# A gather of 1 MB taken apart: U rows first, V rows later and only where the GELU is not zero

## The chip, the cores and the metric

The kernel runs on one core of one Trainium2 chip. The metric is the device time of one execution in microseconds (us). A core has five engines that run on their own and wait for each other by semaphores: TensorE (PE in the profile; PEld is its weight load), VectorE (DVE), ScalarE (ACT), GpSimd (POOL) and SyncE (SP). Sixteen DMA engines move data between HBM and SBUF. SP issues the plain loads here, POOL the indirect ones (gathers).

## The reference, cut to what matters

Four layers work on 256 tokens of width 1024. Each layer is a token mixer (HGRN2, FoX, Mamba-2 SSD, HGRN2) followed by an expert network (PEER). Per token the expert network picks 16 of 16,384 experts for each of 8 heads; an expert has one row of `u_tab` and one of `v_tab`, 1024 floats each:

```python
top_s, pos = lax.top_k(cand_s, PEER_TOPK)
idx = jnp.take_along_axis(cand_i, pos, axis=-1)
gates = jax.nn.softmax(top_s, axis=-1)
u = jnp.take(u_tab, idx, axis=0)
v = jnp.take(v_tab, idx, axis=0)
act = jax.nn.gelu(jnp.einsum('md,mhkd->mhk', xb, u), approximate=False) * gates
return jnp.einsum('mhk,mhkd->md', act, v)
```

So an expert contributes `GELU(x · u) · gate · v`. Where the GELU is zero, the row of V adds nothing. All is float32. The input of the expert network is a normalised vector times a weight near 7.294.

## The kernel before, in words

The 256 tokens are two tiles of 128; four layers by two tiles make eight stages `s` (0 to 7). A stage has 8 heads with 8 pairs of experts each (`NQ`), so 64 iterations; 512 in all (`i` in the main loop at line 1724). One iteration serves one pair of experts of one head for all 128 tokens of the tile: 256 rows. They come by two gathers, `g` = 0 and 1; each brings 128 rows, one to a partition: 64 tokens by 2 experts, `g` being the half of the tokens. The two tables lie side by side in HBM (`uv`): one row is 8 KB, the 1024 floats of U and then those of V. So a gather is 128 rows of 8 KB, 1 MB.

What an iteration does, in program order:

- `fetches(i)` (line 1560): POOL issues gathers until 7 of them are ahead (7 buffers of 1 MB, `NGB`). A gather waits until its buffer is free, which is when the matmuls of the iteration that used it are over.
- `dot(i, 0)`, `dot(i, 1)` (line 1570): DVE multiplies the U half by the tokens (`XR`) and sums each row: one scalar per partition, in tile `dots`.
- `spread(i)` (line 1596): ACT takes the GELU of the two columns, scales the two diagonals `dg` (the gates on a 128 by 64 pattern `m64`) by it, and PE adds the diagonal times the V half into the sum of this stage, a pair of PSUM banks (`acc`): four matmuls, for two halves of the columns and two `g`.
- `others()` and `products_()`: side work for the next tile, of `side(s)`, in small steps: the mixer, the norms, the query projections of stage `s + 1`. `products_` puts PE work in, `others` its evacuation one iteration later. All of it has to be over at iteration 62 of the stage.
- `route_steps`: DVE's top-16 searches that give the indices (`ix`) and gates (`gs`) of heads to come.

Each engine runs its own queue in program order. Nothing is sorted by a scheduler. Three pools of PSUM exist: `ps` (4 banks), `pj` (2 banks, projections of the side work) and `acc` (2 banks, the sum of the stage). The first steps of a stage's side work read the sum of the stage before from `acc`.

Semaphores of gathers go round: the program gives the gathers eight semaphores by turn, so that a gather also waits for the gather eight before it to have landed.

In the last stage more buffers exist (`END`, line 1544): the mixer's room is free then, and up to 19 gathers are ahead.

Of the kernel before, what the change touches and what calls it, by code (L numbers as in the profile page):

```python
# [10 lines left out]
F32 = mybir.dt.float32  # L11
# [17 lines left out]
NGB = 7  # L29
NRAW = 2  # L30
# [17 lines left out]
SPAN = 56  # L48
MOST = ((3.6, 2), (3.5, 2), (3.5, 2), (3.5, 2), (99, 0), (99, 0), (2.8, 2), (3.5, 2))
# [125 lines left out]
def trunk(ctx: ExitStack, tc: tile.TileContext, d: dict, out: bass.AP):  # L175
# [6 lines left out]
    pjp = ctx.enter_context(tc.tile_pool(name="pj", bufs=2, space=SB))  # L182
    accp = ctx.enter_context(tc.tile_pool(name="acc", bufs=2, space=SB))
# [60 lines left out]
    pe = [0.0]  # L244

# [175 lines left out]
    def project(nm, ub, names):  # L421

        for key in names:
            b = pjp.tile([P, 512], F32, name="pj")
# [6 lines left out]
    def out_project(nm, yT, acc):  # L431

        n = len(yT)
        for g in range(n // 4):
            for e in range(2):
                if g == 0:
                    acc.append(pjp.tile([P, 512], F32, name="pj"))
# [761 lines left out]
    def queries(s):  # L1199
# [32 lines left out]
        def alone():  # L1232

            b = pjp.tile([P, 512], F32, name="pj")
# [32 lines left out]
    def pair(s, g, tokens, QT):  # L1267

        l = s // 2
        b = pjp.tile([P, 512], F32, name="pj")  # L1270
# [29 lines left out]
    def late_queries(p, l):  # L1300
# [19 lines left out]
        for i, g in enumerate(gs):  # L1320
# [3 lines left out]
            def start(g=g, made=made):  # L1324
                made["all"] = pair(2 * l, g, tokens, QT)
# [12 lines left out]
    def tail_queries(s, QT):  # L1338

        ready_ = None  # L1340
        for g in (2, 3):
            steps, evac, score = pair(s, g, xT, QT)
# [13 lines left out]
    def beside(norm, work):  # L1356

        for _ in work:
            next(norm, None)
            yield  # L1360
            if deferred:
                flush()
            next(norm, None)
            yield
# [27 lines left out]

    def route(s, hh):
# [15 lines left out]
        igv = ig.rearrange("p c (q j) -> p c q j", j=2)  # L1409
        places = [(slice(j * 64, j * 64 + 64), g, slice(g * 64, g * 64 + 64), j) for g in range(2) for j in range(2)]  # L1410
# [28 lines left out]
        if (s, hh) == (0, 0):  # L1439
# [13 lines left out]
            for o, g, i, j in places:  # L1453
                vec.tensor_copy(ix[o, g, 0:4], igv[i, 0, 0:4, j])
            got[s, hh] = ix, gs, 4
            yield
            for dv, di, src in sides:
# [15 lines left out]
            for o, g, i, j in places:  # L1473
                vec.tensor_copy(ix[o, g, 4:8], igv[i, 0, 4:8, j])
# [4 lines left out]
        else:  # L1479
# [11 lines left out]
            for o, g, i, j in places:  # L1491
                vec.tensor_copy(gs[o, g], igv[i, :, :, j])
            vec.tensor_copy(ix, gs[:, :, 0])
# [46 lines left out]
    accs = {}  # L1540
    sent = [0]
# [4 lines left out]
    def buffer(n):  # L1546

        return GB[n % NGB] if n < LAST else END[(n - LAST) % len(END)]

    def fetch(n):  # L1550
        (s, hh, q), g = pairs[n // 2], n % 2
# [225 lines left out]
```

## Time and profile before

| what | value |
|---|---|
| time, median of 3 runs | 3115.72 us (3115.51 to 3116.24) |
| the profiled execution | 3115.31 us, its span 3113.5 us |
| granted TensorE clock, mean | 0.906 |
| busy share of the span: PE, PEld, DVE, ACT, POOL | 79%, 37%, 68%, 46%, 39% |
| moved by DMA | 1269.42 MB, 408 GB/s on the mean |
| of it by gathers | 1073.81 MB |

The profile is of one execution. Its parts give the busy time of each engine, the span in 40 slices, the DMA queues, the chain of work that ended last, the costliest groups of instructions, and the DMA issues. Other views cut the span into windows, list waits (who waited, for whom, total, number of times, longest), or list instructions in order of time. Queue q0 holds POOL's gathers, q1 SP's loads. A packet of 4 bytes at the end of each DMA on each of the 16 engines signals completion.

### The profile page before, as it was taken

Reading aid. Unit: us, or ns where it says so; the run is one execution under the profiler, and the core shown is the slowest. Engines: PE = TensorE matmul, PEld = TensorE weight load, DVE = VectorE, ACT = ScalarE, POOL = GpSimd, SP = SyncE. Lnnn points to the kernel's source line nnn. Section 1 sums busy time; section 2 is a strip of 40 time slices with the busy share of each in tenths; the row PEclk is TensorE's granted clock in tenths of the full one; section 3 lists DMA queues with packets and bytes.
Section 4 is the critical chain, followed back from the end, with each engine's and each line's share of the span. In section 5 each row is a group of like instructions: output and inputs, shape, how many; then the busy total and the mean of one; then the engine's idle time right before and its main releaser. Section 6 shows DMA issues by size and latency. Waiting matters only on the chain.

```text
span 3113.5 us, 32398 instructions
## 1 busy us (share of the span) xinstructions
PE 2475.0 (79%) x9490; PEld 1153.5 (37%) x9490; DVE 2109.1 (68%) x5580; ACT 1427.1 (46%) x3915; POOL 1200.0 (39%) x1032
## 2 busy tenths in 40 slices
PE   9889768877689777988778998688777898876555
PEld 4434324333235434444233543243323353342222
DVE  1676666667766858678676777577657667776764
ACT  2354334454344634587334674355433544343332
POOL 0243344334443344333343333334334343445443
PEclk9999989988799988999889999899989999888888
DMA  7799999999999999999999999999999999999998
GB/s 310 286 421 403 421 415 404 421 421 419 416 417 418 416 419 408 419 421 412 420 402 421 394 421 421 401 415 421 421 416 411 402 420 421 414 418 416 421 421 345
DMA packets 175710, 1269.42 MB, mean 408 GB/s; under 512 B 19504, under 2 KB 20144, under 8 KB 21296
## 3 DMA queue, kind: packets, MB, share of 16 engines
q0 software_dynamic: 147456, 1073.81, 83.8%
q1 hardware_dynamic: 28080, 193.55, 15.0%
q8 instruction: 78, 1.28, 0.2%
q14 instruction: 96, 0.79, 0.1%
HBM read 1266.23 MB, written 1.05 MB: 407 GB/s over the span
## 4 chain that ended last, share of the span: by engine, by line
DMA 45%; PE 27%; DVE 10%; issue 9%; ACT 5%; POOL 3%; POOLq 0%; DVEq 0%; ACTq 0%
DMA arena<-in_uv,ix 45%; PE acc L1613 12%; PE pj L248 10%; DVE arena L213 8%; PE ps L248 3%; POOL arena L1552 3%; ACT L226 2%; ACT dg L226 2%; ACT arena L226 1%; PE ps L252 1%; ACT dots L226 1%; DVE si L213 0%; DVE cs L213 0%; DMA raw<-in_ssm 0%; DVE sv L213 0%
## 5 line engine op out<-in xcount | busy, mean ns | idle before, releaser
L1552 POOL DMA_INDIRECT arena<-in_uv,ix x1024 | 1196.0, 1168 | 1883.6 <-PE acc L1613 1297.2
L213 DVE SCALAR_TENSOR_TENSOR arena<-arena 128x1024 f32<-128x1024 f32 (+3 forms) x1282 | 1318.4, 1046 | 750.5 <-DMA arena<-in_uv,ix 698.7
L1613 PE MATMUL acc<-arena,dg 128*64 128x512 f32 x4096 | 1266.9, 708 | 611.6 <-ACT dg L226 610.5
L1613 PEld LDWEIGHTS acc<-arena,dg 128*64 128x64 f32 x4096 | 449.7, 152 | 1245.4 <-ACT dg L226 929.9
L226 ACT ACTIVATE dots<-dots 128x2 f32<-128x2 f32 x512 | 103.3, 202 | 1462.8 <-DVE arena L213 1462.3
L248 PE MATMUL pj<-arena 128*128 128x128 f32 (+1 forms) x1752 | 510.1, 440 | 2.0 <-DVE arena L213 1.2
L226 ACT ACT_TABLE_LOAD x339 | 434.9, 1283 | 6.9 <-DVE arena L213 0.8
L248 PE MATMUL pj<-raw,arena 128*128 128x512 f32 x808 | 387.0, 615 | 11.0 <-DMA raw<-in_ssm 8.3
L248 PEld LDWEIGHTS pj<-arena 128*128 128x128 f32 x1752 | 259.4, 193 | 258.8 <-issue 237.9
L226 ACT ACTIVATE dg<-dg,dots 128x64 f32<-128x64 f32 x1024 | 300.4, 340 | 16.7
L226 ACT ACTIVATE dg<-m,gs 128x64 f32<-128x64 f32 x1024 | 292.5, 333 | 0.0
L248 PEld LDWEIGHTS pj<-raw,arena 128*128 128x128 f32 x808 | 145.6, 193 | 248.7 <-issue 222.1
L248 PE MATMUL ps<-arena 128*128 128x128 f32 (+6 forms) x1120 | 149.7, 287 | 1.2 <-ACT arena L1242 1.2
L248 PEld LDWEIGHTS ps<-arena 128*128 128x128 f32 (+3 forms) x1120 | 117.9, 171 | 77.6 <-issue 46.5
L213 DVE MAX8 sv<-arena 128x8 f32<-128x128 f32 x256 | 62.5, 290 | 38.7 <-ACT arena L1228 22.0
L213 DVE DVE_READ_ACCUMULATOR arena<-arena 128x1 f32 x1024 | 84.5, 83 | 0.0
L252 PEld LDWEIGHTS ps<-fst,arena 128*128 128x128 f32 x504 | 60.6, 147 | 62.3 <-issue 35.8
L252 PE MATMUL ps<-fst,arena 128*128 128x128 f32 x504 | 80.0, 288 | 1.3 <-DVE arena L213 1.3
L226 ACT ACTIVATE arena<-arena 128x128 f32<-128x128 f32 (+2 forms) x133 | 67.0, 546 | 18.0 <-DVE arena L213 15.6
L213 DVE FIND_INDEX8 si<-sv,arena 128x8 uint32<-128x128 f32 x256 | 69.8, 285 | 0.0
L248 PEld LDWEIGHTS ps<-fst,arena 128*64 128x64 f32 (+2 forms) x704 | 56.4, 154 | 15.1 <-issue 8.2
L248 PE MATMUL ps<-cst,arena 128*128 128x128 f32 (+2 forms) x256 | 61.7, 358 | 0.0
(119 smaller groups left out, 1291.6 us busy)
## 6 DMA issues: line engine op xcount, KB each, us to landing
raw<-in_ssm SPq DMA_DIRECT2D x48, 1024.0 KB, 9.3
raw<-in_hg SPq DMA_DIRECT2D x35, 1024.0 KB, 9.5
arena<-in_wq SPq DMA_DIRECT2D x28, 1024.0 KB, 9.5
arena<-in_hg SPq DMA_DIRECT2D x27, 1024.0 KB, 15.9
arena<-in_uv,ix POOLq DMA_INDIRECT x1024, 12.0
raw<-in_fox SPq DMA_DIRECT2D x14, 1024.0 KB, 9.8
arena<-in_fox SPq DMA_DIRECT2D x9, 1024.0 KB, 13.7
raw<-in_wq SPq DMA_DIRECT2D x8, 1024.0 KB, 10.4
```

Source lines behind the costliest of these rows:

```text
L213: return getattr(nc.vector, name)(o, *a, **k)
L226: nc.scalar.activation(o, i, f, **k)
L248: nc.tensor.matmul(o, w, m, start=start, stop=stop)
L252: nc.tensor.transpose(o, i, ident)
L1552: nc.gpsimd.indirect_dma_start(buffer(n), None, d["uv"], bass.IndirectOffsetOnAxis(ap=got[s, hh][0][:, g, q:q + 1], axis=0))
L1613: nc.tensor.matmul(accs[s][e][g * 64:g * 64 + 64], dg[:, g], v, start=False, stop=hh == 7 and q == NQ - 1)
```

## The change

The first gather of an iteration stays as it is. The second (`g` = 1) is taken apart for all but the last four iterations (`apart(i)`, 508 of 512): `fetch(i, 1)` brings U rows alone, 128 rows of 4 KB, from the same table seen as rows of half the length (`halved`). V follows in a third gather, `rest_of(i)`. Its index comes from `ask(i)`: two DVE instructions that read the GELU of column 1 and, where it is exactly zero, add a number (`FAR`) beyond the bound of the table; the gather is given that bound and leaves such rows out. What was in the buffer stays there, and is multiplied by zero. `rest_of(i)` is issued one iteration later, and its rows are added in `spread(i + 3)` (`LAG`), ahead of that iteration's own first rows.

The 14 half buffers are divided anew: four of 8 KB a partition for first gathers, three halves for U and three for V. At the end, the four whole second gathers go to the mixer's room, and `END` is gone. Since the index of a U row is twice that of a whole row, `route` doubles those of `g` = 1.

ACT makes the diagonal of the second half later (`diagonal`), from the product of GELU and gate.

Since a stage's last V rows are added three iterations into the next stage, its sum is needed longer. So the pairs of banks `acc` and `pj` swap roles from stage to stage, and the side work that reads the sum waits until iteration 2 of a stage (`LAG - 1`). Work that needs no sum (the last query projections, `tail_queries`) comes ahead of it in the stages where it exists, and in a few iterations at the start of a stage two steps are taken instead of one (`TWICE`).

```diff
+NW = 4
+NH = 3
+LAG = 3
+FAR = 1 << 18
+TWICE = ((3, 4, 5), (1, 2, 3, 4, 5))
...
+    def pj():
+        return (accp, pjp)[(now[0] // 64 + 1) % 2].tile([P, 512], F32, name="pj")
...
+    def apart(i):
+
+        return i < 64 * STAGES - 4
...
-    LAST = 2 * NQ * 8 * (STAGES - 1) + 2 * 16
-    END = [GB[(LAST + k) % NGB] for k in range(NGB)] + [mix[:, o:o + 2 * D] for o in range(3 * D, MIX - 2 * D + 1, 2 * D)]
...
+    halved = d["uv"].rearrange("e (h d) -> (e h) d", h=2)
+    HALF = [at_["gb"][:, (2 * NW + i) * D:(2 * NW + i + 1) * D] for i in range(2 * NH)]
+    def buffer(i, g):
+
+        if not g:
+            return GB[i % NW]
+        if apart(i):
+            return HALF[i % NH]
+        return mix[:, (3 + 2 * (i % 4)) * D:(5 + 2 * (i % 4)) * D]
...
+    def ask(i):
+
+        s, hh, q = pairs[i]
+        a, w = acts[i], asks.setdefault(i, wk2.tile([P, 1], I32, name="ask", bufs=3))
+        vec.tensor_scalar(a[:, 5:6], a[:, 3:4], 0.0, float(FAR), op0=OP.is_equal, op1=OP.mult)
+        stt(w, a[:, 5:6], 1.0, got[s, hh][1][:, 1, 0, q:q + 1], op0=OP.add, op1=OP.add)
+
+    def rest_of(i):
+
+        nc.gpsimd.indirect_dma_start(HALF[NH + i % NH], None, halved, bass.IndirectOffsetOnAxis(ap=asks.pop(i), axis=0),
+                                     bounds_check=2 * DEPTH * P * P - 1, oob_is_err=False)
...
+        while sent[0] < len(jobs_):
+            i, g = jobs_[sent[0]]
+            if pairs[i][2] >= known(i) or i >= n + (NH if g else NW):
+                break
+            if n - 1 in asks and not g:
+                rest_of(n - 1)
+            fetch(i, g)
+            sent[0] += 1
...
+        act(a[:, 2:4], a[:, 0:2], AF.Gelu)
...
+        if i >= LAG and apart(i - LAG):
+            add_rows(i - LAG, 1)
+        for g in range(1 + two):
+            add_rows(i, g)
...
+        while s and now[0] < 64 * s + LAG - 1:
+            yield "wait"
...
-            new, end = i % 64 == 0 and s > 0, i % 64 == 63 and s + 1 < STAGES
+            new, end = i % 64 in TWICE[s % 2] and s > 0, i % 64 == 63 and s + 1 < STAGES
...
             others()
+            if apart(i):
+                ask(i)
```

Three places show how instructions move. The first is POOL's queue in the middle of the program (`arena<-in_uv` is a gather into a buffer; DMASW is a semaphore of an earlier gather; DVE and PE are waits for those engines). Before, two gathers of 128 by 2048 floats an iteration:

```order
L1552 DMA arena<-in_uv,ix 128x2048 [waits DMASW1_49,DVE_49,PE_49]
L1552 DMA arena<-in_uv,ix 128x2048 [waits DMASW2_49,DVE_49,PE_49]
L1552 DMA arena<-in_uv,ix 128x2048 [waits DMASW3_49,DVE_49,PE_49]
L1552 DMA arena<-in_uv,ix 128x2048 [waits DMASW4_49,DVE_49,PE_49]
L1552 DMA arena<-in_uv,ix 128x2048 [waits DMASW5_49,DVE_49,PE_49]
```

With the change, three an iteration: U of iteration n + 2, V of n - 1 (index `ask`), and the whole rows of n + 3:

```order
L1571 DMA arena<-in_uv,ix 128x1024 [waits DMASW7_49,DVE_49]
L1583 DMA arena<-in_uv,ask 128x1024 [waits DMASW0_49,DVE_49,PE_49]
L1571 DMA arena<-in_uv,ix 128x2048 [waits DMASW1_49,PE_49]
L1571 DMA arena<-in_uv,ix 128x1024 [waits DMASW2_49,DVE_49]
L1583 DMA arena<-in_uv,ask 128x1024 [waits DMASW3_49,DVE_49,PE_49]
L1571 DMA arena<-in_uv,ix 128x2048 [waits DMASW4_49,PE_49]
```

The gather of U needs no wait for PE any more, since its buffer is free after the dot product; the gather of V waits for DVE's `ask`, and the whole rows of n + 3 stand behind it. There are 1,024 gathers before, and 1,532 now.

The second place is DVE's queue in one iteration with routing work. Before (the two 128x1024 instructions are the dot products):

```order
L213 TENSOR_TENSOR cs<-cs,sf 128x512 [waits DVE_49]
L213 SCALAR_TENSOR_TENSOR arena,dots<-arena 128x1024 [waits DMASW4_49]
L213 SCALAR_TENSOR_TENSOR arena,dots<-arena 128x1024 [waits DMASW5_49]
L213 TENSOR_TENSOR st<-st 128x1 [waits Activation_49]
L213 TENSOR_REDUCE af<-cs 128x32 [waits DVE_49]
```

With the change, in an iteration with the same routing work:

```order
L218 TENSOR_TENSOR cs<-cs,sf 128x512 [waits DVE_49]
L218 SCALAR_TENSOR_TENSOR arena,dots<-arena 128x1024 [waits DMASW3_49]
L218 SCALAR_TENSOR_TENSOR arena,dots<-arena 128x1024 [waits DMASW4_49]
L218 TENSOR_TENSOR arena<-pj,arena 128x512 [waits PE_49] x2
L218 TENSOR_SCALAR dots<-dots 128x1 [waits Activation_49]
L218 SCALAR_TENSOR_TENSOR ask<-dots,gs 128x1 [waits DMASW5_49,DVE_49]
L218 TENSOR_REDUCE af<-cs 128x32
```

The two new instructions of `ask` stand behind the side work's evacuation (here two additions that wait for PE) and ahead of the routing; they wait for ACT.

The third place is PE's queue. Before, two iterations with side work between them:

```order
L1613 MATMUL acc<-arena,dg 64x512 [waits DMASW0_49,Activation_49]
L1613 MATMUL acc<-arena,dg 64x512 [waits DMASW1_49,Activation_49]
L1613 MATMUL acc<-arena,dg 64x512 x2
L252 MATMUL ps<-fst,arena 128x128 [waits PE_49,Activation_49]
L252 MATMUL ps<-fst,arena 128x128 x3
L1613 MATMUL acc<-arena,dg 64x512 [waits DMASW2_49,Activation_49]
```

With the change (`dh` is the diagonal of the second half):

```order
L1641 MATMUL pj<-arena,dh 64x512 [waits DMASW2_49,Activation_49]
L1641 MATMUL pj<-arena,dh 64x512
L1641 MATMUL pj<-arena,dg 64x512 [waits DMASW0_49,Activation_49]
L1641 MATMUL pj<-arena,dg 64x512
L257 MATMUL ps<-arena 128x128 [waits Activation_49]
```

There are four matmuls an iteration as before, but the first two now wait for the V rows of three iterations earlier.

More of the change, by code (lines that the diff above doesn't have):

```diff
@@ L1265, in queries, with pair @@
                 yield "wait"
-    def pair(s, g, tokens, QT):
+    def pair(s, g, tokens, QT, b):
         l = s // 2
-        b = pjp.tile([P, 512], F32, name="pj")
         ws = []
@@ L1324, in start @@
             def start(g=g, made=made):
-                made["all"] = pair(2 * l, g, tokens, QT)
+                made["all"] = pair(2 * l, g, tokens, QT, pj())
             def step(made=made, start=start):
@@ L1341, in tail_queries @@
         for g in (2, 3):
[L1342 removed]
+            steps, evac, score = pair(s, g, xT, QT, bank())
             for k in range(2):
@@ L1354, in tail_queries, with ahead @@
         yield
-    def beside(norm, work):
+    def ahead(work):
         for _ in work:
-            next(norm, None)
             yield
-            if deferred:
-                flush()
-            next(norm, None)
+            flush()
             yield
@@ L1581, in begin @@
     def begin(s):
-        accs[s] = [accp.tile([P, 512], F32, name="acc") for _ in range(2)]
+        accs[s] = [(accp, pjp)[s % 2].tile([P, 512], F32, name="pj") for _ in range(2)]
         for e in range(2):
@@ L1629, in ready @@
                 nc.sync.dma_start(al(n), d[name])
-        norm = normed(h, t, acc, l, xn, alone=True)
-        if s and t == 0:
-            o = MIX - 5 * UNIT
-            yield from beside(norm, tail_queries(s - 1, mix[:, o:o + 512].rearrange("p (g t) -> p g t", g=4)))
-        yield from norm
+        yield from normed(h, t, acc, l, xn, alone=True)
         if s and t == 0:
@@ L1651, in ready @@
             deferred.clear()
-            warm(1, accp.tile([P, 512], F32, name="acc"), zeros)
+            warm(1, accp.tile([P, 512], F32, name="pj"), zeros)
             for _ in range(5):
@@ L1659, in side @@
     def side(s):
-        if s + 1 < STAGES:
+        last = s + 1 == STAGES
+        if s % 2:
+            o = MIX - 5 * UNIT
+            yield from ahead(tail_queries(s, (spare_of(s + 1)[:, 0:512] if last else mix[:, o:o + 512])
+                                          .rearrange("p (g t) -> p g t", g=4)))
+        while s and now[0] < 64 * s + LAG - 1:
+            yield "wait"
+        if not last:
             yield from ready(s + 1, accs.pop(s - 1) if s else None)
@@ L1674, in trunk @@
     nc.vector.memset(zeros, 0.0)
-    warm(3, accp.tile([P, 512], F32, name="acc"), zeros)
+    warm(3, accp.tile([P, 512], F32, name="pj"), zeros)
     act(spare, eps, AF.Sqrt)
```

88 lines of the change are left out of this document (48 added, 40 removed).

## The prediction

> **What bounds the kernel now.** I read the DMA part of the page first, because half of the chain that ended last is DMA.
>
> ```profile
> span 3113.5 us, 32398 instructions
> DMA  7799999999999999999999999999999999999998
> q0 software_dynamic: 147456, 1073.81, 83.8%
> q1 hardware_dynamic: 28080, 193.55, 15.0%
> DMA 45%; PE 27%; DVE 10%; issue 9%; ACT 5%; POOL 3%; POOLq 0%; DVEq 0%; ACTq 0%
> ```
>
> Gathers and loads together keep the sixteen DMA engines busy for 83.8 + 15.0 = 98.8% of the span. The windows, one for each stage and a last one for what follows the last landing, say it more sharply (the columns end with the granted clock, the DMA share and GB/s):
>
> ```profile
> 113.00:493.00 380.00, 302.18 (x1073) 131.34 (x1071) 265.13 (x733) 165.84 (x458) 149.93 (x132) 0.91 1.00 413
> 493.00:859.00 366.00, 282.65 (x1075) 129.47 (x1073) 251.23 (x685) 163.65 (x478) 150.76 (x128) 0.86 1.01 416
> 1220.00:1631.00 411.00, 341.82 (x1345) 161.43 (x1343) 301.86 (x831) 232.48 (x584) 148.07 (x129) 0.93 1.01 414
> 1631.00:2039.00 408.00, 349.94 (x1383) 167.72 (x1380) 290.15 (x776) 218.82 (x561) 150.65 (x128) 0.92 1.01 412
> 2778.00:3102.00 324.00, 204.36 (x720) 90.22 (x717) 209.78 (x480) 108.48 (x366) 151.61 (x125) 0.83 1.00 414
> 3102.00:3114.00 12.00, 4.08 (x13) 1.50 (x11) 3.14 (x7) 4.49 (x11) 0.00 (x0) 0.88 0.12 45
> ```
>
> From 113 to 3102 us, 2989 us or 5.84 us for each of 512 iterations, the DMA engines are full; even the fullest stage of PE has 58 us of 408 left. The waits agree:
>
> ```profile
> POOL arena L1552 <- PE acc L1613: 1297.2, 406, 9.7
> DVE arena L213 <- DMA arena<-in_uv,ix: 698.7, 528, 4.6
> POOL arena L1552 <- DVE arena L213: 270.6, 66, 111.2
> ```
>
> DVE waits for rows 698.7 us, 1.36 us an iteration; POOL waits for buffers, that is, it would ask for more if it had room. So the time is the DMA engines' work, plus 113 us ahead of the first gather and some 11 behind the last. Only that work can shorten it, and everything else counts only if it leaves the DMA engines idle.
>
> **What the change does to that work.** First the price of a row. All of q0: 83.8% of 16 x 3113.5 engine-us is 41,746, over 131,072 rows of 8 KB (1,024 gathers of 128; the other 16,384 packets signal completion) 318.5 ns. A row of 4 KB is moved in one plain load of 128 such rows, `in_x`, which shares this window of 13.2 us with gathers:
>
> ```profile
> q0 software_dynamic: 687, 4.99, 90.3%
> q1 hardware_dynamic: 144, 0.52, 9.7%
> arena<-in_x SPq DMA_DIRECT2D x1, 512.0 KB, 9.7
> ```
>
> There q1 takes 9.7% of 211.2 engine-us, 20.5 for 128 rows: 160.0 ns. And q0 takes 190.7 for 4.99 MB, 609 rows: 313.1 ns. The ratio is 0.511, so at the whole run's price a row of 4 KB is 162.8 ns. Both hold their share of completion packets.
>
> - Splitting: 508 x 128 = 65,024 rows of 318.5 become two halves of 162.8. That is 7.1 ns a row more, 462 engine-us, **+28.9 us**.
> - Leaving rows out: of the 65,024 V halves a share z goes, each worth 162.8 ns: 661.6 us times z. The share is not in the trace. The reference, evaluated on its own inputs, gives the dot products for tokens 64 to 127 of each tile a spread of 7.30 about zero. Where 1 + erf is rounded to zero in float32 (under about -5.5) lie 22.6% of them; where the exact product underflows (under about -13.2), 3.5%. These are my bounds. Neither is nearer to anything measured, so I take the middle, z = 13%: **-86.0 us**.
> - Unequal engines: a skipped row relieves one engine of sixteen. Each loses about 528 rows by chance, with a spread of 21; the unluckiest of sixteen stands some 38 rows (1.8 spreads) behind. That is 6 us if the last row always waits for that engine, and nothing if the stages even it out. I take **+3 us**.
>
> Sum: 28.9 - 86.0 + 3 = -54 us.
>
> ScalarE's tables have a say in z: the Trainium skill, "ScalarE activation tables: per-element evaluation and per-set limits", section What a function is on this engine, says that beyond a threshold one saturation cubic answers for all inputs, so that an exact zero may begin long before underflow; it names no threshold for GELU and no row here shows one.
>
> **What lies beside it.** The rest costs nothing as long as it stays under 5.73 us an iteration (5.84 less 54/508), and here is the cover of each.
>
> ```profile
> L213 DVE SCALAR_TENSOR_TENSOR arena<-arena 128x1024 f32<-128x1024 f32 x1024 | 1243.3, 1221 | 749.2 <-DMA arena<-in_uv,ix 698.7 <-ACT dg L226 43.7 <-ACT arena L1316 2.6
> L213 DVE RECIPROCAL gt<-gt 128x1 f32<-128x1 f32 x64 | 10.0, 157 | 1.1 <-ACT ig L226 1.0
> L213 DVE TENSOR_SCALAR gt<-ts 128x1 f32<-128x1 f32 x64 | 9.8, 153 | 0.0
> L226 ACT ACTIVATE dg<-dg,dots 128x64 f32<-128x64 f32 x1024 | 300.4, 340 | 16.7
> L1552 POOL DMA_INDIRECT arena<-in_uv,ix x1024: 932/968/2842, 112.9 to 3082.9; - x171
> issue: 121.1, 359
> DMA to landing us min/median/max: 5.8/12.0/28.5
> ```
>
> - DVE: `ask` is two instructions on one column. Such columns cost 153 and 157 ns, so 0.31 us an iteration, 157 us in all, out of the 1.36 us in which DVE waits for rows. Without that cover it would be +157 us. Doubling the indices (62 small instructions) is 10 us more under the same cover.
> - ACT has five small calls a pair before and after; the diagonal scaled by the GELU (340 ns) gives way to a single column. PE has four matmuls as before.
> - POOL: three gathers instead of two. At the mean of 1.17 us (1196.0 over 1024 in the page) and 0.34 us between two (121.1 over 359) that is 4.5 us of 5.73. It fits, but with 1.2 us left.
> - The new wait. Behind V of n - 1, which waits for `ask`, stand the whole rows of n + 3 on POOL, and for those DVE waits three iterations later. These rows show when POOL was let go before:
>
> ```profile
> 1501.81 1.23 DVE L213 SCALAR_TENSOR_TENSOR arena<-arena 128x1024 f32<-128x1024 f32 x1 [1.26 <-DMA arena<-in_uv,ix]
> 1503.07 0.20 ACT L226 ACTIVATE dots<-dots 128x2 f32<-128x2 f32 x1 [2.62 <-DVE arena L213]
> 1503.71 2.17 PE L1613 MATMUL acc<-arena,dg 128*64 128x512 f32 x8
> 1505.91 0.94 POOL L1552 DMA_INDIRECT arena<-in_uv,ix  x1 [3.32 <-PE acc L1613]
> ```
>
> The second dot ends at 1503.04, PE lets go at 1505.88, 2.8 us later. `ask` comes after GELU and one evacuation on DVE, mostly before that; then V's 1.17 us on POOL. The whole rows are asked for about 1 us later than now, while U is asked for some 2.8 us earlier. What lies ahead of them in the queue when U of n - 1 has landed: the rest of three iterations, at 2.55 + 1.30 + 1.13 = 4.98 us of gathering each, more than 11 us. The wait for the gather eight before leaves as much: eight by turn are 8/3 of an iteration's, 13.3 us. So the engines do not run dry, whereas losing 0.11 us an iteration would eat the whole gain (54/508).
> - V of n - 3 lands right behind U of n in the same queue, 1.1 us later. PE needs it after the dot (1.22), GELU and one diagonal, about 1.9 us later: just in time, and a late one holds up only the next buffer.
> - The later start of a stage's side work, 2 to 4 iterations: at the end of a stage it has room. Windows of the projections (tile `pj`, PE first) before the ends of stages 2, 3 and 5:
>
> ```profile
> 1172.00:1208.00 36.00, 0.00 (x0) 0.00 (x0) 0.00 (x0) 0.00 (x0) 0.81 1.00 409
> 1580.00:1615.00 35.00, 0.00 (x0) 0.00 (x0) 0.00 (x0) 0.00 (x0) 0.85 0.98 393
> 2360.00:2398.00 38.00, 0.00 (x0) 0.00 (x0) 0.00 (x0) 0.58 (x1) 0.87 1.01 414
> ```
>
> Some 35 us, six iterations, hold none; and the doubled steps make the order catch up. Without that cover, seven stages by three iterations would be 21 x 5.8 = 122 us.
> - Fewer buffers in the last stage: it was full at 1.00 with 19 gathers ahead, but so were the others at 1.00 and 1.01 with 7. Nothing.
>
> The profiled execution took 3115.31 us against the median of 3115.72, 0.4 less; the sum from it is 3115.3 - 54 = **3061 us**.
>
> **The rivals.** (a) *The skip saves little or nothing*: the GELU is hardly ever exactly zero, or a row outside the bound occupies an engine as a moved one does. Nothing in the trace speaks against it, since no gather of before has a bound. At z = 0: 3115.3 + 28.9 + 3 = 3147 us, slower; it decides below z = 4.8%, where the skips no longer pay for the split.
>
> (b) *POOL becomes the bound.* Place: POOL's queue, three gathers an iteration. A gather took 0.97 us at the median and 2.84 at most; whether the bound makes V's dearer is unknown. At 2.84 us the iteration is 2 x 1.51 + 2.84 + 0.34 = 6.20 us, and 512 of them with 113 and 11 around give 3298 us. It decides from 5.73 - 3.02 - 0.34 = 2.4 us for V's gather. Against it: the bound is one comparison a row, beside writing a row's descriptor, which the 0.97 us already hold 128 times.
>
> (c) *The queue runs dry at times*, since the whole rows stand behind `ask` where the side work is heavy, in the stages with 302 and 290 us of DVE in 411 and 408. If 128 iterations lose 0.23 us each, that is 29 us: 3090 us, half the gain.
>
> (d) *More zeros*, z = 22.6%: 661.6 x 0.226 = 149.5; 3115.3 + 28.9 - 149.5 + 3 = 2998 us.
>
> (e) *Each further transfer costs its fixed part in the open.* A store of 256 KB into an idle queue took 2.3 us:
>
> ```profile
> out<-arena SPq DMA_DIRECT2D x4, 256.0 KB, 2.3
> ```
>
> Its bytes are half of `in_x`, 10.3 engine-us or 0.6 us over sixteen engines, so about 1.7 us are fixed; 508 times in the open is 864 us, 3925 us in all. Against it: `in_x` took 9.7 us to land and 1.3 us (20.5/16) of the engines, the rest ran beside other rows. The Trainium skill, "DMA: Bandwidth & Descriptors", section Rules for kernel authors, asks for 1 MiB and more a DMA, and its section Anatomy of one DMA puts about 2.0 us of fixed cost to each; by that, 508 x 2.0 = 1016 us would be added, and the shares of 1.00 in the windows disagree while a queue stands.
>
> **How the numbers follow.** The forecast has 0.68, (a) 0.12, (b) 0.06, (c) 0.10, (d) 0.03, (e) 0.01. The predicted time is the forecast's, 3061 us. At the bottom, z = 16% (-20) with rows of 160.0 ns unscaled (121,595 of them, 2.8 ns less, -21) gives 3020; at the top, z = 3.5% (+63) gives 3124. So 3020 to 3125; (b), (e), the bottom of (d) and z = 0 stay outside. A change under 0.2%, 6.2 us, can't be told from none. Faster: forecast, (c) and (d), 0.81, less a little for z near 5%: 0.80. Same 0.04. Slower 0.16.
>
> **What would show it.** Right: DMA share still 0.99 to 1.01 in all eight stages; moved bytes down by 65,024 x 0.13 x 4 KB = 34.6 MB, to about 1235 MB; q0's packets near 187,600 rows of data; stages 7 us shorter each; POOL busy about 60% of the span; DVE's wait for rows down by some 200 us with no new wait of its length. Wrong: bytes as before (then a); POOL without idle time (then b); windows with a DMA share of 0.97 and less in the stages of 411 and 408 us (then c).

## The result, and the profile after

| | median, us | lowest to highest | against the kernel before |
|---|---|---|---|
| before, beside it | 3115.98 | 3115.51 to 3118.19 | 1 |
| with the change | 3099.16 | 3094.97 to 3101.28 | 0.9943 (95% interval 0.9926 to 0.9960) |

The change makes the kernel 17 us faster, where the prediction had 54. The time lies inside the range, but less than a third of the gain arrived. The profiled execution took 3099.7 us. The runs below were made in groups, each with the kernel before beside it (medians 3115.98 to 3118.18 us); a ratio is to that one.

The page of the changed kernel, its span, its DMA parts and its chain:

```profile
span 3097.7 us, 35191 instructions
DMA packets 248883, 1235.71 MB, mean 399 GB/s; under 512 B 35921, under 2 KB 36561, under 8 KB 159472
q0 software_dynamic: 220608, 1039.92, 83.5%
q1 hardware_dynamic: 28080, 193.55, 15.3%
DMA 38%; PE 32%; DVE 18%; ACT 3%; issue 3%; POOL 1%; POOLq 0%; DVEq 0%
```

The bytes are what was forecast, 1235.7 MB. q0's 220,608 packets are 66,048 rows of 8 KB, 121,759 rows of 4 KB and 32,801 packets of 4 bytes. Of the latter 1,532 x 16 = 24,512 signal completion; the other 8,289 stand where a row was left out. So z is 8,289 of 65,024, 12.75%, almost the 13% assumed. Yet q0's work fell only from 83.8% of 3113.5 (2609 us) to 83.5% of 3097.7 (2587 us), 22 us in place of 57. These shares add up the packets' times, also where more than sixteen packets are under way at once. Counted from the packets of the trace, one engine to a packet, from the first packet of a gather to the end of the last, the time beyond sixteen is 53.7 us (37.7 before), and engines stood unused for 33.3 us (17.3 before), each as a time of all sixteen.

The windows of four stages (columns as before: at the end granted clock, DMA share and GB/s):

```profile
121.00:490.00 369.00, 314.19 (x1085) 125.23 (x1086) 279.54 (x850) 160.32 (x455) 220.45 (x192) 0.96 1.02 412
1211.00:1623.00 412.00, 358.34 (x1336) 158.80 (x1336) 316.06 (x959) 222.06 (x574) 218.62 (x193) 0.94 1.01 406
1623.00:2034.00 411.00, 365.17 (x1394) 167.19 (x1392) 309.49 (x927) 215.31 (x560) 220.21 (x193) 0.94 1.00 399
2763.00:3082.00 319.00, 221.32 (x655) 79.31 (x652) 223.18 (x600) 102.31 (x356) 200.52 (x183) 0.89 1.00 404
```

The DMA share stands at 1.00 to 1.02, before at 1.00 to 1.01, but the rate in the last column has fallen: 406 and 399 GB/s in the stages that had 414 and 412, 404 in the last one that had 414. By the share the engines are as busy, and they move less. A good part of that is the price of the split, which the prediction had counted: the kernel with the split alone (first experiment) has 410, 407 and 410 in these stages.

The waits of the changed kernel (who waited for whom, total us, times, longest):

```profile
DVE arena L218 <- DMA arena<-in_uv,ix: 390.5, 249, 4.7
POOL arena L1583 <- PE pj L1641: 366.9, 223, 7.1
PE pj L1641 <- DMA arena<-in_uv,ask: 342.6, 193, 7.8
POOL arena L1583 <- DMA arena<-in_uv,ix: 116.9, 57, 5.1
```

DVE's wait for rows went down by 308 us. New is PE's wait for V (`in_uv,ask`), 342.6 us at 193 places, and POOL's wait ahead of V's gather (L1583), for the matmuls that free V's buffer, 366.9 us. Everything that POOL issues later stands behind that. A wait of POOL is a loss only where the DMA engines run out of rows meanwhile: before, POOL waited 1297.2 us for PE, and the engines were full. And while POOL stood there, PE was seldom waiting for a V row itself: of the 366.9 us, by the trace, PE waited for V in 15, did side work in 97, and worked at the sums of rows (L1641) in 253.

The stages one by one, from a stage's first dot product to the next stage's, the last to the end (us; the kernels of the later columns are the experiments below):

| stage | before | change | split only | all rows | all rows, steps by stage | no doubled steps | steps apart | steps by stage |
|---|---|---|---|---|---|---|---|---|
| 0 | 379.5 | 369.4 | 382.3 | 375.9 | 377.8 | 369.0 | 369.2 | 371.0 |
| 1 | 363.1 | 361.4 | 369.9 | 372.3 | 371.1 | 360.9 | 362.8 | 359.1 |
| 2 | 363.3 | 360.1 | 370.5 | 369.2 | 368.9 | 358.9 | 356.1 | 359.2 |
| 3 | 408.3 | 411.7 | 410.9 | 415.9 | 416.2 | 411.3 | 418.6 | 411.5 |
| 4 | 411.0 | 410.6 | 414.0 | 411.5 | 412.7 | 412.0 | 404.9 | 406.9 |
| 5 | 375.2 | 366.6 | 378.1 | 378.7 | 379.3 | 378.1 | 370.6 | 366.7 |
| 6 | 360.8 | 362.6 | 367.6 | 369.6 | 368.1 | 361.2 | 359.3 | 358.7 |
| 7 | 331.7 | 334.7 | 333.1 | 344.4 | 338.5 | 330.9 | 332.5 | 332.0 |

Every stage was to be 7 us shorter. Stages 0 and 5 are 10 and 9 us shorter, 3, 6 and 7 are longer. The table is of one execution of each kernel, and differences of a few us in it say little: the run with six buffers for V (below) differs from the change only in the last stage, and its stage 0 took 375.8 us against 369.4. The executions shown for "no doubled steps" (3107.1 us) and "steps apart" (3099.2) were the fastest of their kernels, whose medians are 3114.0 and 3106.1.

### The profile page after: what moved, and what is told of

It reads as the page before. It is cut to its first block, busy times and chain, and to the rows that moved or that the text cites. A ratio compares the mean times of both kernels' runs of the same rounds, so it can differ in the third digit from the quotient of the medians.

```text
span 3097.7 us, 35191 instructions
## 1 busy us (share of the span) xinstructions
PE 2608.6 (84%) x9490; PEld 1113.6 (36%) x9490; DVE 2250.7 (73%) x6664; ACT 1387.2 (45%) x3898; POOL 1735.0 (56%) x1540
## 2 busy tenths in 40 slices
DMA packets 248883, 1235.71 MB, mean 399 GB/s; under 512 B 35921, under 2 KB 36561, under 8 KB 159472
## 3 DMA queue, kind: packets, MB, share of 16 engines
q0 software_dynamic: 220608, 1039.92, 83.5%
## 4 chain that ended last, share of the span: by engine, by line
DMA 38%; PE 32%; DVE 18%; ACT 3%; issue 3%; POOL 1%; POOLq 0%; DVEq 0%
DMA arena<-in_uv,ask 19%; DMA arena<-in_uv,ix 18%; PE pj L1641 13%; PE pj L257 12%; DVE arena L218 10%; PE ps L257 6%; DVE cs L218 2%; ACT dots L231 1%; DVE si L218 1%; PE ps L261 1%; DVE ti L218 1%; ACT L231 1%; DVE ts L218 1%; DVE ask L218 1%; DVE af L218 1%
## 5 line engine op out<-in xcount | busy, mean ns | idle before, releaser
L1571 POOL DMA_INDIRECT arena<-in_uv,ix x1024 | 1076.4, 1051 | 614.1 <-issue 151.9
L1641 PE MATMUL pj<-arena,dh 128*64 128x512 f32 x2048 | 1085.9, 657 | 382.3 <-DMA arena<-in_uv,ask 342.6
L1641 PE MATMUL pj<-arena,dg 128*64 128x512 f32 x2048 | 1105.0, 667 | 84.5 <-ACT dg L231 83.9
L1583 POOL DMA_INDIRECT arena<-in_uv,ask x508 | 654.5, 1288 | 722.3 <-PE pj L1641 366.9
L1641 PEld LDWEIGHTS pj<-arena,dh 128*64 128x64 f32 x2048 | 255.1, 144 | 929.7 <-issue 668.6
L257 PE MATMUL pj<-arena 128*128 128x512 f32 (+1 forms) x1336 | 459.4, 491 | 2.5 <-DVE arena L218 1.7
L1641 PEld LDWEIGHTS pj<-arena,dg 128*64 128x64 f32 x2048 | 258.0, 146 | 356.9 <-ACT dg L231 196.2
L231 ACT ACTIVATE dg<-dg,dots 128x64 f32<-128x64 f32 x512 | 178.0, 348 | 16.8
L231 ACT ACTIVATE dh<-m,dots 128x64 f32<-128x64 f32 x508 | 169.1, 333 | 12.3 <-PE pj L1641 12.2
L231 ACT ACTIVATE dg<-m,gs 128x64 f32<-128x64 f32 x512 | 170.2, 332 | 0.0
L231 ACT ACTIVATE dots<-dots,gs 128x1 f32<-128x1 f32 x508 | 141.7, 279 | 0.0
L218 DVE SCALAR_TENSOR_TENSOR ask<-dots,gs 128x1 int32<-128x1 f32 x508 | 81.4, 160 | 53.6 <-DMA arena<-in_uv,ask 36.3
L218 DVE DVE_READ_ACCUMULATOR arena<-arena 128x1 f32 x1024 | 84.4, 82 | 0.0
```

What stands on the lines that cost most here:

```text
L218: return getattr(nc.vector, name)(o, *a, **k)
L231: nc.scalar.activation(o, i, f, **k)
L257: nc.tensor.matmul(o, w, m, start=start, stop=stop)
L1571: nc.gpsimd.indirect_dma_start(buffer(i, g), None, halved if g and apart(i) else d["uv"], bass.IndirectOffsetOnAxis(ap=got[s, hh][0][:, g, ...
L1583: nc.gpsimd.indirect_dma_start(HALF[NH + i % NH], None, halved, bass.IndirectOffsetOnAxis(ap=asks.pop(i), axis=0), bounds_check=2 * DEPTH ...
L1641: nc.tensor.matmul(accs[s][e][g * 64:g * 64 + 64], dg, v[:, e * 512:(e + 1) * 512], start=False, stop=hh == 7 and q == NQ - 1)
```

## The experiments

Where could 37 us have gone? Into the split, if it costs more than 29 us; into the new order of the work, which the prediction put at nothing; into uneven engines, if fifteen wait for one; or a left-out row is worth less than its packet. Each of the first four runs takes one part of the change alone. (The theories are numbered within the expectations of each group of runs.)

**The split alone.** The kernel before, with only its second gather split into two gathers of 4 KB rows, both early; nothing is left out, no order is changed.

```diff
 def fetch(n):
     (s, hh, q), g = pairs[n // 2], n % 2
+    if g:
+        for e in range(2):
+            nc.gpsimd.indirect_dma_start(buffer(n)[:, e * D:(e + 1) * D], None, d["uv"].rearrange("e (h d) -> (e h) d", h=2),
+                                         bass.IndirectOffsetOnAxis(ap=got[s, hh][0][:, 1 + e, q:q + 1], axis=0))
+        return
...
```

(Not shown: `route` makes V's indices beside U's, in a wider `ix` with three buffers in place of four. What that costs by itself, no run shows.)

> The kernel before with one edit: the second gather of each pair is two gathers of 4 KB rows, U and V one after the other, both early, with indices known from the routing; same buffers, no ask, no lag, no swap of PSUM pairs. By the prediction's price, 7.1 ns for each split row: 3116 + 29 = 3145 us. Theory 1: as dear as all rows in the changed form, 3179. Theory 3: 3145 to 3150, and all rows in the changed form stand above it by what order and waits cost.

Measured: 3149.43 us, ratio 1.0106 (1.0089 to 1.0123), **+33 us**, against +28.9 in the sum.

```profile
span 3147.1 us, 33517 instructions
q0 software_dynamic: 221184, 1073.84, 84.4%
```

Its windows of stages 3, 4 and 7, beside 414, 412 and 414 GB/s before:

```profile
1243.40:1654.30 410.90, 340.08 (x1311) 158.46 (x1312) 302.45 (x838) 229.93 (x579) 209.96 (x190) 0.95 1.01 410
1654.30:2068.30 414.00, 357.81 (x1396) 167.31 (x1392) 293.33 (x801) 219.12 (x562) 215.11 (x192) 0.93 1.01 407
2814.00:3131.00 317.00, 197.14 (x644) 86.64 (x643) 206.32 (x485) 103.90 (x353) 198.49 (x184) 0.81 1.01 410
```

By the packets of its trace a row of 4 KB takes 163.3 ns (162.8 in the prediction) and one of 8 KB 318.2. q0's time grew by more than the span, 47 us (84.4% of 3147.1 against 2609), because more packets are under way at once: the time beyond sixteen is 55.7 us, before 37.7. The price of the split was read well from `in_x`.

**All rows.** The changed kernel with nothing to leave out: the bound is never passed.

```diff
-FAR = 1 << 18
+FAR = 0
```

> The changed kernel with FAR = 0: no row of V is left out, everything else (three gathers, order, waits) stays. Theory 1, price: the DMA engines stay full and each of the 8,289 left-out rows is worth a 4 KB row less the 4-byte packet that it leaves, 163.8 - 9.3 ns over 16 engines, 80 us: 3099 + 80 = 3179 us. Theory 2, unequal engines: the skips are worth less than their mean, since a gather lands with its slowest engine: 3099 + 60 = 3159 us. Theory 3, waits: the queue runs dry for other reasons and part of the skipped work was idle time anyway: 3099 + 50 = 3150 us or less.

Measured: 3167.58 us, ratio 1.0167 (1.0150 to 1.0184). That gives the ledger of the change: the split +33, the new order (late V, other buffers, side work moved) 3167.6 - 3149.4 = **+18**, the rows left out 3099.2 - 3167.6 = **-68**; together -17. The 3167.6 lies between theories 1 and 2.

```profile
span 3161.7 us, 35191 instructions
q0 software_dynamic: 220608, 1073.84, 84.1%
```

The two profiled executions, all rows and changed, differ by 64.0 us of span (the medians by 68), and the packets of the traces account for it. A left-out row saves 163.8 - 9.3 ns (its 4-byte packet stays), times 8,289 over 16 engines: -80.0 us. The 66,048 rows of 8 KB became dearer, 318.4 to 320.3 ns: +7.8. The time in which engines stand unused between the first and the last gather went from 26.5 to 33.3 us: +6.8. SP's loads: +1.3. Sum -64.1.

**The same number of rows from each engine.** Sixteen fixed rows of each V gather are left out, 8,128 in all, one of each DMA engine if the engine goes by the partition as the Trainium skill, "DMA: Bandwidth & Descriptors", section The descriptor swizzle, says.

```diff
-vec.tensor_scalar(a[:, 5:6], a[:, 3:4], 0.0, float(FAR), op0=OP.is_equal, op1=OP.mult)
-stt(w, a[:, 5:6], 1.0, got[s, hh][1][:, 1, 0, q:q + 1], op0=OP.add, op1=OP.add)
+vec.tensor_scalar(a[:, 5:6], a[:, 3:4], 0.0, 0.0, op0=OP.is_equal, op1=OP.mult)
+stt(w, a[:, 5:6], skip, got[s, hh][1][:, 1, 0, q:q + 1], op0=OP.add, op1=OP.add)
...
```

(Not shown is how `skip` is made: it is 1 + `FAR` in every fourth partition of 0 to 31 and of 64 to 95, else 1.)

> The changed kernel, but the rows left out are 16 fixed partitions of each V gather (every fourth of partitions 0 to 31 and 64 to 95), 8,128 in all, chosen so that every DMA engine is relieved of one row; ask still waits for the GELU. The rows left out are not those of zero GELU, so a part of the sum is missing. Theory 2: the loss by unequal engines vanishes, 15 to 20 us less than the changed kernel: about 3082 us. Theories 1 and 3: as the changed kernel, 3099 + 2 = 3101 us.

Measured: 3107.41 us, ratio 0.9967 (0.9956 to 0.9979), worth 60 us against all rows. Equal shares are no faster than those that the data give, so uneven engines are not the cause. They are even 8 us slower; 161 rows fewer left out explain 1.6 of that, the rest stays open.

**The same number, from two engines.** As before, but partitions 0 to 7 and 32 to 39, which by the same section belong to two engines.

> As the one before, with the 16 rows of each V gather taken from partitions 0 to 7 and 32 to 39, which should belong to two DMA engines alone; again a part of the sum is missing. If the slowest engine sets the pace (theory 2 taken to its end), fourteen engines still move everything and nothing is gained: as with all rows, 3150 to 3180 us. If only the total work counts (theory 1), 3101 us.

Measured: 3164.0 us, ratio 1.0152 (1.0135 to 1.0169), worth 3.6 us against all rows, inside the intervals of the two.

```profile
span 3162.2 us, 35193 instructions
q0 software_dynamic: 220608, 1040.58, 82.6%
```

As many rows are left out as in the run before, and the time is that of all rows: the slowest engine sets the pace, and the engine follows from the partition. The two times agree with that section for gathers too; the profile does not name the engine of a packet.

**More rows.** Rows of V are also left out where the GELU is about 1e-7 and less, by a threshold on the dot product.

```diff
-vec.tensor_scalar(a[:, 5:6], a[:, 3:4], 0.0, float(FAR), op0=OP.is_equal, op1=OP.mult)
+vec.tensor_scalar(a[:, 5:6], a[:, 1:2], -5.5, float(FAR), op0=OP.is_lt, op1=OP.mult)
```

> The changed kernel with another test in ask: rows are left out where the dot product is under -5.5 instead of where the GELU is exactly zero, so the rows left out carry a GELU of 1e-7 and less. By the reference that is 22.6% of the rows instead of 12.75%, 6,400 more. If the DMA engines' work alone sets the time: 6,400 x 154.5 ns / 16 = 62 us less, 3037 us. Theory 3 (the queue runs dry more, the less there is to move; all rows to zero rows gave 68 of 80): 0.6 to 0.85 of it, 3047 to 3062 us.

Measured: 3036.8 us, ratio 0.9746 (0.9731 to 0.9761).

```profile
span 3031.0 us, 35429 instructions
DMA packets 248885, 1209.56 MB, mean 399 GB/s; under 512 B 42316, under 2 KB 42956, under 8 KB 159472
q0 software_dynamic: 220608, 1013.75, 83.2%
```

6,395 more rows are left out (42,316 - 35,921), and 62 us are gained: 6,395 x 154.5 / 16 = 61.8. In this order of the work these rows are worth their full packet, so the work of the DMA engines does set the time. That does not hold in every order: with the doubled steps apart, and with steps by stage (both below), the same 6,395 rows were worth 53.6 us (3106.05 to 3052.41) and 51.5 us (3089.15 to 3037.62), 0.87 and 0.83 of their packets, about the share that the 8,289 rows had (68 of 80). Whether something is lost once or with each row is thus not settled.

**Does the ask hold up V?** With the fixed rows of the equal skip, `ask` needs no GELU and is put right behind the first dot product.

```diff
-vec.tensor_scalar(a[:, 5:6], a[:, 3:4], 0.0, 0.0, op0=OP.is_equal, op1=OP.mult)
+vec.tensor_scalar(a[:, 5:6], eps, 0.0, 0.0, op0=OP.is_equal, op1=OP.mult)
...
 dot(i, 0)
+if apart(i):
+    ask(i)
...
 others()
-if apart(i):
-    ask(i)
```

> As the equal skip (16 fixed rows of each V gather left out), but ask no longer reads the GELU and stands ahead of the dot products, so that POOL never waits for it. If the wait for ask is what empties the queue: 10 to 18 us less than the equal skip's 3107, 3090 to 3097 us. If it is not (POOL's V gather is let go by PE, which frees its buffer, 366.9 us of waits against 32.3 for ask): 3107 us.

Measured: 3107.24 us, ratio 0.9971 (0.9959 to 0.9983), against 3107.41 with the late `ask`. The wait for `ask` costs nothing.

**Buffers in the last stage.** The two profiled executions of all rows and of the split alone are 14.6 us of span apart, and 11 of these lie in stage 7 (344.4 and 333.1). From its iteration 16 on, V gets six buffers in the mixer's room instead of three.

```diff
+def vroom(i):
+    if i >= 64 * (STAGES - 1) + 16:
+        return mix[:, (11 + i % 6) * D:(12 + i % 6) * D]
+    return HALF[NH + i % NH]
...
```

> The changed kernel with six buffers for V rows instead of three, in the mixer's room, from iteration 16 of the last stage on; so the gather of V(i) no longer waits for the matmuls of iteration i to free its buffer. Nothing else differs. If the three V buffers hold up POOL and with it the queue (theory 3; PE waits 86.6 us for V rows in the last stage, and the last stage is 11 us longer with all rows than in the split-only form), the last stage shortens by 5 to 10 us: 3090 to 3094 us. If the last stage's loss is its tail or the price of rows: 3099 us.

Measured: 3098.61 us, ratio 0.9938 (0.9923 to 0.9952): no change. The number of V's buffers there is not the loss; the start of the stage, ahead of iteration 16, is not touched by this run, and more room there for whole rows and for U, which the change took away too, was not run.

**Own rows first.** PE adds the first rows of an iteration ahead of the late V rows, not behind them.

```diff
-if i >= LAG and apart(i - LAG):
-    add_rows(i - LAG, 1)
 for g in range(1 + two):
     add_rows(i, g)
+if i >= LAG and apart(i - LAG):
+    add_rows(i - LAG, 1)
```

> The changed kernel with the order of PE's matmuls in an iteration turned: the iteration's own first rows are added ahead of the V rows of three iterations before. If PE's wait for late V rows (342.6 us) holds up the buffers of the first rows and so the queue: 5 to 15 us less, 3085 to 3094 us. If V rows are in time often enough, or the order only shifts the wait: 3099 us.

Measured: 3110.74 us, ratio 0.9977 (0.9967 to 0.9988), slower than the change by about 11, which neither theory has. POOL's wait ahead of V's gather for PE is 480.2 us, with the change 366.9. Freeing V's buffer first is the better order, which points at that buffer.

**V one iteration earlier.** PE needs V one iteration sooner. (The same constant also lets the side work that reads the sum start one iteration sooner.)

```diff
-LAG = 3
+LAG = 2
```

> The changed kernel with V added two iterations later instead of three (LAG = 2); nothing is left out. A gather takes 12.2 us from its issue to landing, 2.1 iterations of 5.8 us, and V's is issued one iteration after its ask, so that PE meets V about an iteration too early. The prediction's view (a late V holds up only the next buffer, and the queue covers it): PE's wait for V grows from 342.6 us to over 1000, and the time stays at 3099 to 3110. Rival: the late matmuls hold the buffers of whole rows and of V, POOL issues later, the DMA engines run dry: 0.5 us and more an iteration, over 3350.

Measured: 3147.96 us, ratio 1.0084 (1.0065 to 1.0102), **49 us** slower than the change. Its waits, and the window from the first dot product to the last gathers, followed by the same window of the changed kernel:

```profile
POOL arena L1571 <- PE pj L1641: 625.3, 312, 9.4
PE pj L1641 <- DMA arena<-in_uv,ask: 495.1, 243, 8.2
ACT dh L231 <- PE pj L1641: 337.6, 177, 7.6
122.00:3130.00 3008.00, 2418.97 (x8996) 1048.92 (x8996) 2199.23 (x6552) 1370.99 (x3819) 1735.15 (x1530) 0.92 1.00 400
```

```profile
121.00:3082.00 2961.00, 2484.46 (x8992) 1047.18 (x8992) 2211.52 (x6541) 1341.95 (x3811) 1727.09 (x1528) 0.94 1.01 406
```

Neither number expected came: a late V is not free, as the prediction's view had it, nor does it cost half a microsecond an iteration; it costs a tenth. The rival has the place right: the gather that waits is now that of the whole rows (L1571), 625.3 us for PE against 27.7 with the change. The loss does not show in the DMA share (1.00 and 1.01), but in the rate. By the packets, unused time grew by 11.9 us, rows of 8 KB went from 320.3 to 325.6 ns, which is 22 us, and rows of 4 KB from 163.8 to 164.8, which is 8.

**Where the side work stands.** The rows around a stage's start show how POOL comes to wait for PE. This is the changed kernel at the start of stage 7 (start, duration, engine; in brackets the idle time before and who ended it):

```profile
2768.16 7.41 PE L257 MATMUL ps<-arena 128*128 128x128 f32 x64
2768.88 1.68 POOL L1583 DMA_INDIRECT arena<-in_uv,ask  x1 [1.21 <-DVE ts L218]
2770.87 0.94 POOL L1571 DMA_INDIRECT arena<-in_uv,ix  x1 [0.30 <-issue]
2772.11 0.94 POOL L1571 DMA_INDIRECT arena<-in_uv,ix  x1 [0.30 <-DVE ti L218]
2775.51 0.64 PE L1641 MATMUL pj<-arena,dh 128*64 128x512 f32 x1
2777.71 1.00 POOL L1583 DMA_INDIRECT arena<-in_uv,ask  x1 [4.66 <-PE pj L1641]
2788.14 0.99 POOL L1583 DMA_INDIRECT arena<-in_uv,ask  x1 [6.95 <-PE pj L1641]
```

64 small matmuls of the side work fill PE from 2768.2 to 2775.6. The matmuls that free V's buffer (`dh`) stand behind them, POOL waits 4.66 us for those, and ten microseconds later 6.95 us: for that long no gather at all is issued. The doubled steps of `TWICE` put such blocks into successive iterations. Two runs take them away or apart (one line in each):

```diff
-TWICE = ((3, 4, 5), (1, 2, 3, 4, 5))
+TWICE = ((), ())                          # the first run
+TWICE = ((4, 9, 14), (4, 9, 14, 19, 24))  # the second
```

> The changed kernel with no doubled steps at the start of a stage (TWICE empty); nothing is left out of the computation, the side work is only spread. Theory 1: at the start of a stage PE works through side work in blocks of 64 small matmuls (7.4 us at 2768 us), the matmuls that free V's buffer stand behind it, V's gather waits for them (4.7 and 7.0 us at 2777 and 2788 us), and all gathers stand behind V's on POOL. Then the unused DMA time in the 40 us from 500, 2430 and 2780 us (3.4 + 2.3 + 3.9 us) goes by more than half, and the time is 5 to 10 us under the changed kernel's 3099, about 3091. Theory 2: the doubled steps are not the cause, the late matmuls of V are late anyway: 3099 +/- 3. Theory 3: without the doubled steps the work bunches up later in the stage: slower, 3104 and more.

> The changed kernel with its doubled steps apart: iterations 4, 9, 14 and 4, 9, 14, 19, 24 of a stage in place of 3, 4, 5 and 1 to 5. Nothing is left out of the computation. Theory 1 (blocks of side work right behind one another hold up V's buffer and with it all gathers): about 3093, between the changed kernel and the one without doubled steps. Theory 2 (not the cause): 3099 +/- 3. Theory 3: slower, 3104 and more.

Measured: 3113.98 us without them, ratio 0.9988 (0.9980 to 0.9997), and 3106.05 apart, 0.9963 (0.9951 to 0.9976): slower than the change, by 15 and 7 (the interval of the second just overlaps that of the change). So theory 3, that the work then bunches up later, holds for the sum. Windows say that theory 1, the blocks at the start, holds for the starts. Three windows, the starts of stages 1 and 7 and the change from stage 4 to 5, of the changed kernel and of that without doubled steps, and at last the two starts in the kernel before:

```profile
490.00:530.00 40.00, 38.42 (x212) 23.66 (x210) 26.71 (x73) 17.24 (x48) 20.50 (x19) 1.00 0.92 359
2000.00:2040.00 40.00, 29.47 (x135) 12.51 (x133) 34.44 (x116) 15.44 (x47) 24.63 (x23) 0.87 0.99 378
2765.00:2800.00 35.00, 31.26 (x192) 21.20 (x193) 24.63 (x68) 17.24 (x48) 17.92 (x18) 0.98 0.87 322
```

```profile
490.00:530.00 40.00, 35.38 (x211) 21.77 (x207) 29.08 (x82) 15.17 (x47) 24.64 (x23) 0.98 0.99 383
2000.00:2040.00 40.00, 25.56 (x123) 10.74 (x122) 28.18 (x98) 12.94 (x40) 18.59 (x19) 0.88 0.74 280
2765.00:2800.00 35.00, 34.05 (x246) 23.12 (x247) 28.61 (x79) 14.32 (x45) 21.62 (x19) 1.00 0.99 380
```

```profile
500.00:540.00 40.00, 39.53 (x234) 24.81 (x234) 26.60 (x63) 18.25 (x52) 16.04 (x14) 1.00 0.98 389
2784.00:2819.00 35.00, 30.50 (x193) 20.18 (x193) 24.94 (x56) 18.25 (x52) 13.56 (x13) 0.98 1.01 403
```

Without doubled steps the starts of stages 1 and 7 are as full as before the change (0.92 and 0.87 become 0.99), but around 2020 us the share falls from 0.99 to 0.74, where POOL issued 19 gathers instead of 23. So the gain at the start of a stage is lost at the end of another; that it is the delayed side work which costs the time there was argued, not tested.

The steps apart went also into the kernel that leaves more rows out:

> The run with more rows left out (those of a dot product under -5.5) together with the doubled steps of a stage apart. V's rows whose GELU is about 1e-7 and less are left out. Theory 1: as much faster than 3036.8 as the spread steps alone are than the changed kernel, about 3030. Theory 2: 3037 +/- 3. Theory 3: slower than 3041.

Measured: 3052.41 us, ratio 0.9792 (0.9777 to 0.9807), slower than its like (3036.8) by 16; again the steps apart lose in the sum.

**Steps chosen by stage.** None in stages 1 and 7, apart in 2, 4 and 6, the change's own in 3 and 5; with the rows left out as the change does, with none left out, and with more.

```diff
-TWICE = ((3, 4, 5), (1, 2, 3, 4, 5))
+TWICE = ((), (), (4, 9, 14), (1, 2, 3, 4, 5), (4, 9, 14), (1, 2, 3, 4, 5), (4, 9, 14), ())
...
-new, end = i % 64 in TWICE[s % 2] and s > 0, i % 64 == 63 and s + 1 < STAGES
+new, end = i % 64 in TWICE[s] and s > 0, i % 64 == 63 and s + 1 < STAGES
```

> The changed kernel with the doubled steps chosen for each stage by what the two runs before showed: none in stages 1 and 7, iterations 4, 9, 14 in stages 2, 4 and 6, the change's own 1 to 5 in stages 3 and 5. Nothing is left out. Theory 1 (a stage loses where its side work bunches, at its start or at its end, and a stage's loss is its own): the stages come out as in the best of the three runs, 360.9, 356.1, 411.7, 404.9, 366.6, 359.3 and 330.9 us, 17 us under the changed kernel: 3082 (3078 to 3088). Theory 2 (time lost in one stage moves to the next, the sum stays): 3099 +/- 4.

> The same steps by stage with no row left out, so that all of V is moved. It stands against the run of all rows (3167.6) and the run of the split alone (3149.4), which are 18 us apart, the price of the order that the prediction put at nothing. Theory 1 (that price is the bunching of the side work): about 3152, the split alone. Theory 2 (it is the late V itself, whatever the steps): 3165 and more. The distance to the run before it in this call is the worth of the rows left out: 80 us by their packets, 68 as found so far.

> The same steps by stage with the rows left out whose dot product is under -5.5 (V rows whose GELU is about 1e-7 and less are left out). Theory 1: 17 us under 3036.8, about 3020. Theory 2: 3037 +/- 4.

Measured: 3089.15 us, ratio 0.9910 (0.9897 to 0.9924), 10 under the change and 29 under the kernel before beside it, with the computation whole; 3158.13 with all rows, ratio 1.0133 (1.0117 to 1.0148), 9.5 under its like; 3037.62 with more rows left out, 0.9743 (0.9730 to 0.9757), no gain over 3036.8 (theory 2 there). Of the first, neither theory came: 10 us were gained of the 17 that the best stages of three executions had promised. Best stages picked out of single executions that scatter by some us promise too much; how much of the 7 that is, no run shows. The last stage with all rows, first as the change orders it, then with steps by stage:

```profile
2817.00:3146.00 329.00, 216.12 (x655) 83.63 (x655) 224.05 (x604) 103.45 (x360) 200.92 (x183) 0.87 1.00 405
```

```profile
2817.00:3140.00 323.00, 216.61 (x659) 81.40 (x657) 224.09 (x603) 103.74 (x360) 199.44 (x183) 0.83 1.01 412
```

So half of the order's +18 is where the side work stands, and it is unused DMA time: by the packets 26.5 us of it became 22.2 with all rows (21.4 with the split alone), and 33.3 became 24.2 with the change's rows, most of the 6.0 and 9.8 us that the two spans lost. The other half stays open. The gain does not add to that of more rows; why, the runs don't tell. The worth of the left-out rows is 69 us under this order, as under the other, so its missing 11 us do not come from the bunching. Combinations beyond these weren't tried.

## Why the prediction was right in kind and wrong in size

The prediction missed 37 us. Two of its terms hold nearly all of it: the rows left out were worth 18 us less than it had, and the new order, which it put at nothing, cost 18. The split cost 4 more, and the 3 for uneven engines did not come.

- **The bound: right.** Moving less is what shortens the kernel: 6,395 rows more brought 0.83 to 1.0 of their packets, by the order of the work.
- **Splitting, +28.9: right**, +33.
- **Rows left out, -86.0: the share was right, the worth was not.** z was 12.75% for 13%, which takes off 1.6. That the share came so close was luck: 13% was the middle between two bounds with nothing measured between them. The working took a left-out row to cost nothing; it keeps a packet of 9.3 ns, 4.8 us in all. That leaves -80, and -68 was measured. In the two profiled executions the rest is rows of 8 KB that became 1.9 ns dearer (7.8 us) and 6.8 us more of unused engines. What makes the rows dearer is not settled.
- **The range, 3020 to 3125,** was made from the share and the price of a row alone, and the share came out near its middle. That the time lies in it says nothing for the terms that failed.
- **Unequal engines, +3: not to be seen.** Equal shares were not faster. That the slowest engine sets the pace is shown by the run on two engines.
- **`ask` under DVE's wait and ahead of the whole rows: right** as far as `ask` goes (3107.24 and 3107.41). **POOL: right**, 56% busy; rivals (a), (b), (d) and (e) fall.
- **"A late one holds up only the next buffer": this step failed.** "Just in time" was half right: PE waited for V 193 times, 342.6 us in all, up to 7.8. The step that failed is what follows from it. V's gather is in one queue with all the others and waits there for its buffer, which PE frees; whatever makes PE's V matmuls late stops every gather behind it (4.66 and 6.95 us at the start of stage 7). With the change that was mostly PE's own work, side work at these places, and not V's landing (15 of 366.9 us). The more than 11 us of queued rows that were to cover it did not suffice: the share fell to 0.87 there, and one iteration less for V costs 49 us.
- **The later start of the side work, at nothing: wrong.** Room at the end of a stage was the cover. The prediction showed it for the ends of stages 2, 3 and 5. The line below is the same view of the kernel before towards the end of stage 4: projections are still at work there, and the share is under 1 already. That is where the kernel without doubled steps runs dry. With them the price is at the starts, where they stand ahead of V's matmuls. Steps by stage give back half of the order's +18.

```profile
2000.00:2026.00 26.00, 2.02 (x5) 0.57 (x3) 0.00 (x0) 0.59 (x1) 0.87 0.96 370
```

- **The last stage, "Nothing": wrong**, some 11 us longer with all rows than with the split alone, though not for want of V's buffers from iteration 16 on; steps by stage give back 5.9 of them.
- **Rival (c)**, 3090, came nearer than the forecast. It named the stages 3 and 4, and these gave the least: leaving rows out was worth 4.2 and 0.9 us there, and 7.0 to 12.1 in the others but one (6.5). Its sign, a share of 0.97 and less, did not come; the loss was in GB/s. That sign was badly chosen: the share counts packets that are under way beyond sixteen (53.7 us), and so it stands at 1.00 while engines are unused (33.3 us).
- **"No new wait of its length": wrong**, 342.6 us on PE.

The sum, mended: +33 for the split, -68 for the rows, +18 for the order, -17 in place of -54.

## What to carry to other kernels

A transfer that waits for its buffer in a queue with others delays all of them; when one is put there whose buffer an engine with other work has to free, count what that engine has to do before that buffer is free, at the starts of stages above all. Read the moved GB/s beside the DMA share: a share of 1.00 went with 414 and with 399 GB/s here, of which the shorter rows explain a part. And when a change carries a compensation of its own (the doubled steps), try that stage by stage: it was worth 10 us here, though not together with more rows left out.

## What the runs showed of the hardware

A row outside a gather's bound still leaves a packet of 4 bytes, 9.3 ns on its engine instead of 163.8. For POOL a gather with the bound takes longer, as the view of the tile shows (durations in ns, smallest, median and largest; L1583 has the bound):

```profile
L1571 POOL DMA_INDIRECT arena<-in_uv,ix x1024: 932/937/1995, 112.2 to 3070.9; - x171
L1583 POOL DMA_INDIRECT arena<-in_uv,ask x508: 993/1304/2093, 124.7 to 3066.9; - x170
```

At the least it is 0.99 us against 0.93, so the bound itself costs about 0.06 (an estimate). The medians, 1.30 and 0.94, differ by more, but not for the bound alone: with V one iteration earlier, the same gathers with the same bound have a median of 1.00 us. The zeros of ScalarE's GELU are 12.75% of inputs with a spread of 7.30 about zero; if these are normally distributed, the exact zero begins near 1.14 spreads, -8.3 (an estimate), between the two bounds of the prediction. And a row of 8 KB took 317.3 ns before, 320.3 with the change and 325.6 with V an iteration earlier, while the engines' share stayed full: the duration of a packet is not a constant of its size.
